# Giving every room a length that is a multiple of 128 bytes, and a planner's durations taken from the trace

## The chip, the cores and the metric

The kernel runs on one core of one Trainium2 chip. The metric is the device time of one execution in microseconds (us); lower is better. An execution is one launch that computes the whole reference.

## The reference

Two macaron layers over x, 256 tokens by 1024 features, all in float32. Each layer is a SwiGLU feed-forward, a mixer, and a second feed-forward, each closed by a LayerNorm. The mixer is a bidirectional mLSTM in layer 0 and a windowed attention in layer 1.

```python
def swiglu(x, w_in, w_out):            # w_in 1024 x 5632, w_out 2816 x 1024
    gu = x @ w_in
    g, u = gu[..., :D_FF], gu[..., D_FF:]
    return (jax.nn.silu(g) * u) @ w_out

for l in range(2):
    x = layer_norm(ALPHA * x + 0.5 * swiglu(x, ffn_w_in[l, 0], ffn_w_out[l, 0]), ...)
    y = mlstm_mixer(x, ...) if l == 0 else window_attention(x, ...)
    x = layer_norm(ALPHA * x + y, ...)
    x = layer_norm(ALPHA * x + 0.5 * swiglu(x, ffn_w_in[l, 1], ffn_w_out[l, 1]), ...)
```

Nearly all of the work is in four feed-forwards of 256 tokens with 17.3 million weights each.

## The kernel before, in words

**Products.** Each float32 matrix is split in two parts that TensorE takes as float32r: `hi`, the value rounded by a cast on ScalarE (ACT), and `lo`, the rest, by a subtraction on VectorE (DVE). A product is three matmuls (`mm3`): hi·hi, hi·lo, lo·hi. In nearly all of them the weights are the moving operand, 128 x 512 (`w_hi`, `w_lo`), and the activations are the stationary one, 128 x 128: `xT_hi`/`xT_lo` (the transposed x), `h_hi`/`h_lo` and `hc` (the gated activations, called h), `q` (the attention's output) or `S` (sums of blocks of x). The text calls a matmul with 512 moving columns a long product. There are 3447 of them among TensorE's 4459 matmuls.

**Feed-forward.** Columns of `w_in` are taken in blocks. A first block is computed plainly from `xT`; then four calls of `seven`, in which seven block products stand for eight (a Strassen-like scheme: sums of weight blocks are made by DVE and by DMAs that add, issued by GpSimd, POOL). A call of `seven` has 84 long products, 36 of them with `xT` and 48 with `S`, and up to 48 of the down projection (`py<-w,h`), 132 together in the first three of the four calls, 108 in the last, and 8 transposes. Then `tail` does the last of the down projection, the residual and the LayerNorm (`Norm`): half of token tile 1 is computed while tile 0 is normalized, and tile 1 is normalized while the next stage starts.

**Order.** No engine's order is written by hand. `Book` records every step. TensorE keeps the recorded order. For the other queues (ACT, DVE, POOL, and SP, which issues the loads) `sequence` simulates the program: each step has a duration (`takes`) and a time until its result is seen (`later`), both set in `cost`; a step gets a due time from TensorE's order, and the most urgent one that can start is taken.

**Rooms.** SBUF is cut into rooms of the kinds in `HOMES`: (bytes per partition, number of rooms). A step that opens a room waits for a free one of its kind. `hi` and `lo` hold the split weights, 10 each; `big` holds raw weights as loaded, h, S and v; `small` holds statistics. Each room becomes one tile, allocated when it is first used, so that a room's address is the sum of all the lengths before it. The constants `xT_hi` and `xT_lo` stand at bytes 24704 and 32896 of a partition, multiples of 128. Behind them stand the small constants (`mhalf`, `gcol`, `gw`, `gbias`, `sink`, `neg_sink`), 736 bytes in all, and among the rooms small ones of 32 to 96 bytes. Rooms that hold `v` (128 x 4 x 258, 4128 bytes) are not a multiple of 128 long either.

In the built program this is where the operands of the 3447 long products begin, as the remainder of the byte modulo 128:

| moving, stationary | before | after |
|---|---|---|
| 96 and 0 | 1408 | |
| 96 and 96 | 1135 | |
| 96 and 32 | 273 | |
| 32 and 96 | 214 | |
| 32 and 0 | 192 | |
| 96 and 64 | 160 | |
| 32 and 32 | 41 | |
| 32 and 64 | 24 | |
| 0 and 0 | | 3447 |

Before, the two remainders are equal in 1176 long products and differ in 2271; all 1536 long products with `xT` are among the latter.

The program's own scheduling function is the place of the durations that change:

Of the kernel before, what the change touches and what calls it, by code (L numbers as in the profile page):

```python
# [10 lines left out]
F32 = mybir.dt.float32  # L11
# [7 lines left out]
S = 256  # L19
# [6 lines left out]
A = slice(None)  # L26
# [2 lines left out]
HOMES = {  # L29
    "hi": (4096, 10),  # L30
    "lo": (4096, 10),
    "big": (4128, 20),
    "wide": (4352, 2),
    "temp": (2048, 6),
    "small": (80, 20),
# [73 lines left out]
class View:  # L109
# [27 lines left out]
    def real(self):  # L137
        r = self.room.real
        for name, args, kw in self.ops:
            r = getattr(r, name)(*args, **kw)  # L140
        return r
# [23 lines left out]
class Book:  # L165
# [76 lines left out]
    def cost(self, s):  # L242

        size = lambda v: int(np.prod(v.shape[1:]))
        n = max([size(v) for v in s.outs + s.ins], default=0)
        if s.engine == "PE":
            n = size(s.outs[0])
            s.takes, s.later = (109.0 if s.name == "transpose" else n / 2.4 + 13.3), 200.0
            if s.name == "matmul" and s.args[1].shape[0] == 64:
                s.takes = 111.0  # L250
        elif s.name == "dma_start":
            s.takes = {"SP": ISSUE, "ACT": 480.0, "POOL": 1250.0}[s.engine]
            s.later = 0.0
        elif s.engine == "DVE":
            s.takes, s.later = (n + 71) / 0.96, 120.0
            if s.name == "tensor_tensor_scan":
                s.takes = 700.0
            if s.name == "tensor_tensor_reduce":
                s.takes += 60.0
        elif s.engine == "ACT":  # L260
            s.takes, s.later = n * 0.912 + 25.0, 125.0
            if s.name.startswith("preload"):
                s.takes = 1290.0
            if s.name == "activation" and s.args[2] is not AF.Copy:
                s.takes += 30.0
            if "accum_out" in s.kw:
                s.takes += 100.0
        else:
            s.later = 150.0
            s.takes = {"tensor_tensor": 1500.0, "tensor_add": 1000.0, "partition_broadcast": 1100.0, "iota": 600.0,  # L270
                       "affine_select": 1000.0}.get(s.name, n * 0.93 + 60.0)
            if s.name == "tensor_add" and n >= 512:
                s.takes = 2150.0

    def seen(self, s):
        return s.end + s.later
# [148 lines left out]
    def emit(self):  # L425
        nc = self.nc
        engines = {"PE": nc.tensor, "DVE": nc.vector, "ACT": nc.scalar, "POOL": nc.gpsimd, "SP": nc.sync}
        real = lambda x: x.real() if isinstance(x, View) else x
        for s in self.order():
            for r in s.rooms:  # L430
                if r.real is None:
                    pool = self.pools[r.kind == "bank"]
                    r.real = pool.tile(list(r.shape), r.dtype, name=r.name, tag=f"{r.kind}{r.slot}", bufs=1)
            getattr(engines[s.engine], s.name)(*[real(x) for x in s.args], **{k: real(x) for k, x in s.kw.items()})  # L434

# [2 lines left out]
def trunk_kernel(ctx: ExitStack, tc: tile.TileContext, x, ffn_w_in, ffn_w_out, ln_g, ln_b, ml_w_in, ml_gate_b,  # L438
                 ml_norm_g, ml_w_out, at_w_in, at_sink, at_w_out, out):
    consts = ctx.enter_context(tc.tile_pool(name="consts", bufs=1))  # L440
    rooms = ctx.enter_context(tc.tile_pool(name="rooms", bufs=1))
    banks = ctx.enter_context(tc.tile_pool(name="banks", bufs=1, space=bass.MemoryType.PSUM))
    ctx.enter_context(tc.manual_schedule())
    nc = Book(tc.nc, (rooms, banks))

    stages = [("ffn", 0, 0, 0), ("mlstm", 0, 0, 1), ("ffn", 0, 1, 2),
              ("ffn", 1, 0, 0), ("attn", 1, 0, 1), ("ffn", 1, 1, 2)][:STAGES]
# [1 line left out]
    def const(name, shape, dtype=F32):  # L449
        t = consts.tile(list(shape), dtype, name=name)  # L450
        v = nc.tile(name, shape, "const", dtype)
        v.room.real = t
        v.room.slot = 0
        return v
# [4 lines left out]
    def pair(p, *idx):  # L459
        return p[0][idx], p[1][idx]  # L460

    def bank(shape=(128, 512), name="pw"):
        return nc.tile(name, shape, "bank")
# [4 lines left out]
    def small(name, shape):  # L468
        return nc.tile(name, shape, "small")

    def both(name, shape, kind="big"):
        return tuple(nc.tile(name + e, shape, kind, FR) for e in ("_hi", "_lo"))
# [50 lines left out]
    def mm3(o, l, r, start, stop, onto=False):  # L523
        nc.tensor.matmul(o, l[0], r[0], start=start, stop=False, skip_group_check=onto)
        nc.tensor.matmul(o, l[0], r[1], start=False, stop=False, skip_group_check=onto)
        nc.tensor.matmul(o, l[1], r[0], start=False, stop=stop, skip_group_check=onto)
# [11 lines left out]
    xt = [const(f"x{t}", [128, D]) for t in range(2)]  # L538
    xT = tuple(const("xT" + e, [128, 8, S], FR) for e in ("_hi", "_lo"))
    ident = const("ident", [128, 128])  # L540
    mhalf = const("mhalf", [128, 2])
    gcol = const("gcol", [128, 8])
    gw = const("gw", [128, 8, 16])
    gbias = const("gbias", [128, 1])
    sink = const("sink", [128, 16])
    neg_sink = const("neg_sink", [128, 16])

    for t, h in ((0, 0), (1, 0), (0, 1), (1, 1)):
        s_ = slice(h * 512, h * 512 + 512)
# [120 lines left out]
    def ffn(l, i, n, pending, last):  # L670
        wi, wo = ffn_w_in[l, i], ffn_w_out[l, i]
        hT, y = {}, []
        start = pending is None

        def h_room(width):
            if width == 4:
                return both("h", (128, 4, S))
            v = nc.tile("hc", (128, 2, 2, S), "big", FR)
            return v[:, 0], v[:, 1]

# [81 lines left out]
        def x_four():  # L762
            x_sum("S4", turned[0, 1], OP.add, f1["S2"])

        hB = h_room(4)
        chunks(hB, 4)
        hB0 = hB
# [59 lines left out]
        def seven(g, before):  # L827
# [7 lines left out]
            of = lambda k0, t: (lambda k: pair(xT, A, k0 + k, tok(t)))  # L835
            sum_ = lambda name: (lambda k: pair(xs[name], A, k))
            hB = h_room(4)
            chunks(hB, 4)
            qa, qc = bank(), bank()
# [61 lines left out]
        for t in range(2):  # L901
            sg = temp("sg")[:, 0:256]
            nc.scalar.activation(sg, ps[t][:, 0:256], AF.Silu)
            hh.append(temp("hh")[:, 0:256])
            nc.vector.tensor_mul(hh[t], sg, ps[t][:, 256:512])
        hp = h_room(2)
        chunks(hp, 2)
        down(1)
# [17 lines left out]
        return tail(y, lambda c, t: pair(hT[c], A, tok(t)), (todo, todo), False, norm, last, 4, turn)  # L926

    def mlstm(l, n, pending, last):
        va = [both(f"v{t}", (128, 4, 258)) for t in range(2)]
        gwi = both("gw", (128, 8, 128))  # L930
        for p in gwi:
            nc.gpsimd.memset(p.bitcast(F32), 0.0)
# [44 lines left out]
        for d in range(2):  # L977
            q = slice(32 * d, 32 * d + 32)
# [4 lines left out]
        for d in range(2):  # L983
            q = slice(32 * d, 32 * d + 32)
# [39 lines left out]
        for m in range(2):  # L1024
            for g in range(2):
                pieces = [narrow(ml_w_in[0], a * 512, 512 * m + 256 * g) for a in range(2)]
                p = bank((128, 2, S))
# [10 lines left out]
        am = {}  # L1038
# [17 lines left out]
        def mix(h):  # L1056
            den = small("den", (128, 2, 2))
            ys = []
            for t in range(2):
                for d in range(2):  # L1060
                    y = bank(name="py")
                    terms = [(t, t)] if t == d else [(t, t), (2, 1 - t)]
                    for n_, (blk, sb) in enumerate(terms):
                        mm3(y[:, 0:258], pair(am[h], A, d, blk), pair(va[sb], A, h), n_ == 0, n_ == len(terms) - 1)
                    nc.scalar.activation(den[:, t, d:d + 1], y[:, 256:257], AF.Abs)
                    ys.append(y)
            part[h] = den, ys
# [42 lines left out]
        for h in range(4):  # L1110
            wide_mm(po[h // 2], 0, wg, h // 2, range(4 * (h % 2), 4 * (h % 2) + 4))
            scores(h)
            if h:
                mix(h - 1)
                divide(h - 1)
                settle(h - 1)
        po1 = [bank(), bank()]
        sigm(0, 0, po[0])
        wide_mm(po1[0], 1, wg, 0, range(4))
        mix(3)  # L1120
        sigm(0, 1, po[1])
        wide_mm(po1[0], 1, wg, 0, range(4, 8))
# [12 lines left out]
        y = [[bank(name="py") for _ in range(2)] for _ in range(2)]  # L1135
# [10 lines left out]
    def attn(l, n, pending, last):  # L1146
# [18 lines left out]
        va = [nc.tile(f"v{t}", (128, 17, 64), "wide", FR) for t in range(2)]  # L1165
        for t in range(2):
            nc.gpsimd.memset(va[t][:, 0:17:2].bitcast(F32), 0.0)
        kT = both("kT", (128, 4, S))
        qh = [both(f"q{h}", (128, 4, S)) for h in range(2)]
        qT = lambda j, *idx: pair(qh[j // 4], idx[0] if idx else A, j % 4, *idx[1:])  # L1170
        kd, qd = [], []
        wkq = later([lambda c0=c0, a=a: wide(at_w_in[0], a * 256, c0) for c0 in (1024, 0) for a in range(4)])
# [99 lines left out]
        y = []  # L1272
# [53 lines left out]
    for j, (kind, l, i, n) in enumerate(stages):  # L1326
        last = j == len(stages) - 1
        bound[0] = j
        if kind == "ffn":
            pending = ffn(l, i, n, pending, last)  # L1330
        elif kind == "mlstm":
            pending = mlstm(l, n, pending, last)
        else:
            pending = attn(l, n, pending, last)
# [30 lines left out]
```

## Time and profile before

| | |
|---|---|
| median of 3 runs | 941.18 us (941.17 to 941.67) |
| profiled execution | 941.73 us, its span 940.0 us |
| granted TensorE clock | 0.998 |
| TensorE (PE) busy | 919.6 us, 98% |
| VectorE (DVE) busy | 809.6 us, 86% |
| ScalarE (ACT) busy | 584.0 us, 62% |
| GpSimd (POOL) busy | 155.6 us, 17% |
| moved by DMA | 208.54 MB, mean 222 GB/s |

The profile's page gives the busy time of the engines; PEld is the weight load of TensorE (the stationary operand), which overlaps its matmuls (PE). A matmul's record ends about 0.39 us after its start, though the next one starts 0.23 us after it: matmuls overlap in the array. So the cost of a matmul is read from start to start, or from the chain of work, whose pieces are laid end to end. Line numbers in the profile are nearly all L434, the line of `emit` that issues every step; names tell the steps apart.

### The profile page before, as it was taken

What the parts mean: (1) busy time and instruction counts of PE and PEld (TensorE: products, weight loads), DVE (VectorE), ACT (ScalarE), POOL (GpSimd) and SP (SyncE); (2) the same over time, 40 slices, a digit from 0 to 9 for tenths busy, and PEclk for the clock granted to TensorE, in tenths of its full rate; (3) what the DMA queues carried; (4) which work ended last, traced back from release to release, by engine and by line L of the source; (5) the groups of instructions that cost most, each with busy time, mean ns of one, the idle gap of its engine ahead of it and who ended that gap; (6) DMA issues with size and microseconds to landing.
All of it is one profiled execution on the core that took longest, in us unless ns stands there. A gap on an engine that the chain in (4) does not pass through costs nothing.

```text
span 940.0 us, 12633 instructions
## 1 busy us (share of the span) xinstructions
PE 919.6 (98%) x4459; PEld 756.4 (80%) x4459; DVE 809.6 (86%) x969; ACT 584.0 (62%) x793; POOL 155.6 (17%) x194
## 2 busy tenths in 40 slices
PE   8999999999999999999999999999989999999997
PEld 6888888789978888888878888887878878888885
DVE  6979999887788979999789799988776688899975
ACT  6676767548454666676446676675467555776660
POOL 6112111015011012111011112110045302111100
PEclk9999999999999999999999999999999999999999
DMA  9998999854296488988975889988522457989821
GB/s 315 334 258 197 286 283 274 289 183 143 104 369 221 132 211 217 305 275 220 335 246 135 240 215 272 303 264 286 172 74 79 157 202 158 281 241 236 270 46 45
DMA packets 100704, 208.54 MB, mean 222 GB/s; under 512 B 6904, under 2 KB 21264, under 8 KB 100640
## 3 DMA queue, kind: packets, MB, share of 16 engines
q1 hardware_dynamic: 82368, 173.04, 53.2%
q0 software_dynamic: 17696, 33.65, 21.0%
q10 hardware_dynamic: 576, 1.05, 0.3%
q8 instruction: 35, 0.57, 0.3%
q14 instruction: 29, 0.24, 0.1%
HBM read 206.65 MB, written 1.05 MB: 221 GB/s over the span
## 4 chain that ended last, share of the span: by engine, by line
PE 84%; DVE 8%; DMA 3%; issue 2%; ACT 2%; POOL 1%; DVEq 0%; SPq 0%; ACTq 0%; POOLq 0%
PE pw L434 56%; PE py L434 27%; DVE w_lo L434 4%; DMA raw<-in_ffn_w_in_dram 1%; DMA raw<-in_ml_w_in_dram 1%; DVE x L434 1%; ACT w_hi L434 1%; ACT sc L434 1%; DMA raw<-in_ffn_w_out_dram 0%; POOL rs L434 0%; DVE stats L434 0%; DVE b L434 0%; DVE xT_lo L434 0%; DVE sc L434 0%; DVE e L434 0%
## 5 line engine op out<-in xcount | busy, mean ns | idle before, releaser
L434 ACT CAST w_hi<-b 128x1024 fp32r<-128x1024 f32 x224 | 234.1, 1053 | 93.5 <-PE py L434 53.4
L434 DVE TENSOR_TENSOR w_lo<-b,w_hi 128x1024 fp32r<-128x1024 f32 x224 | 267.5, 1219 | 25.4 <-ACT w_hi L434 25.2
L434 ACT CAST w_hi<-raw 128x1024 fp32r<-128x1024 f32 (+1 forms) x181 | 186.8, 1046 | 101.5 <-PE py L434 65.9
L434 DVE TENSOR_TENSOR w_lo<-raw,w_hi 128x1024 fp32r<-128x1024 f32 (+1 forms) x181 | 216.8, 1214 | 33.8 <-ACT w_hi L434 33.3
L434 PE MATMUL pw<-w_hi,xT_hi 128*128 128x512 f32 x480 | 192.1, 401 | 0.1
L434 PE MATMUL pw<-w_hi,xT_lo 128*128 128x512 f32 x480 | 189.4, 396 | 2.8 <-DVE xT_lo L434 2.8
L434 PE MATMUL pw<-w_lo,xT_hi 128*128 128x512 f32 x480 | 189.0, 395 | 1.3 <-DVE w_lo L434 1.3
L434 PE MATMUL pw<-w_hi,S 128*128 128x512 f32 x512 | 164.6, 392 | 0.0
L434 POOL DMA_DIRECT2D b<-in_ffn_w_in_dram x64 | 77.3, 1210 | 465.9 <-DVE b L434 161.4
L434 PE MATMUL py<-w_hi,h_hi 128*128 128x512 f32 x317 | 126.2, 398 | 0.0
L434 PE MATMUL py<-w_hi,h_lo 128*128 128x512 f32 x317 | 124.8, 394 | 0.4 <-DVE h_lo L434 0.4
L434 PE MATMUL py<-w_lo,h_hi 128*128 128x512 f32 x317 | 124.5, 393 | 0.0
L434 PEld LDWEIGHTS pw<-w_hi,S 128*128 128x128 f32 x512 | 96.1, 188 | 21.7
L434 PEld LDWEIGHTS pw<-w_hi,xT_lo 128*128 128x128 f32 x480 | 90.1, 188 | 25.9 <-DVE xT_lo L434 4.5
L434 PEld LDWEIGHTS pw<-w_lo,xT_hi 128*128 128x128 f32 x480 | 90.2, 188 | 21.6 <-DVE w_lo L434 1.7
L434 PEld LDWEIGHTS pw<-w_hi,xT_hi 128*128 128x128 f32 x480 | 90.1, 188 | 20.2 <-ACT w_hi L434 0.6
L434 PE MATMUL pw<-w_lo,S 128*128 128x512 f32 x256 | 100.4, 392 | 0.0
L434 DVE TENSOR_TENSOR b<-b,b 128x1024 f32<-128x1024 f32 x64 | 78.0, 1221 | 1.2
L434 PEld LDWEIGHTS py<-w_hi,h_lo 128*128 128x128 f32 x317 | 59.5, 188 | 14.9 <-DVE h_lo L434 1.1
L434 PEld LDWEIGHTS py<-w_lo,h_hi 128*128 128x128 f32 x317 | 59.6, 188 | 13.0
L434 PEld LDWEIGHTS py<-w_hi,h_hi 128*128 128x128 f32 x317 | 59.6, 188 | 12.6
L434 PEld LDWEIGHTS pw<-w_lo,S 128*128 128x128 f32 x256 | 48.1, 188 | 10.9
(198 smaller groups left out, 1083.1 us busy)
## 6 DMA issues: line engine op xcount, KB each, us to landing
b<-in_ffn_w_in_dram SPq DMA_DIRECT2D x128, 512.0 KB, 6.4
raw<-in_ffn_w_out_dram SPq DMA_DIRECT2D x88, 512.0 KB, 6.8
b<-in_ffn_w_in_dram POOLq DMA_DIRECT2D x64, 512.0 KB, 8.1
raw<-in_ffn_w_in_dram SPq DMA_DIRECT2D x32, 512.0 KB, 7.6
raw<-in_ml_w_in_dram SPq DMA_DIRECT2D x24, 512.0 KB, 6.1
raw<-in_ffn_w_in_dram SPq DMA_DIRECT2D x32, 256.0 KB, 7.3
raw<-in_at_w_in_dram SPq DMA_DIRECT2D x12, 512.0 KB, 8.8
raw<-in_ml_w_out_dram SPq DMA_DIRECT2D x8, 512.0 KB, 4.1
```

The costliest lines, as they stand in the source:

```text
L434: getattr(engines[s.engine], s.name)(*[real(x) for x in s.args], **{k: real(x) for k, x in s.kw.items()})
```

## The change

It has three parts.

1. Rooms. Kinds of length 4128 go: `big` has 16 rooms of 4096 bytes, and a new kind `tall` has 4 of 4224 (33 x 128). `tall` holds h of width 4, v of the mLSTM (now 264 columns a head, of which 258 are read) and q of the attention. The six small constants become parts of one tile `few` of 768 bytes. Small rooms get a pool of their own (`smalls`), allocated behind all the others.
2. Durations in `cost` for DVE, ACT and POOL, which set the order of their queues. None of an instruction's own shape, type or work changes.
3. What follows: the order of DVE, ACT and POOL, and which room a step gets.

TensorE's order and the order of the loads on SP are as before.

```diff
 HOMES = {
     "hi": (4096, 10),
     "lo": (4096, 10),
-    "big": (4128, 20),
+    "big": (4096, 16),
+    "tall": (4224, 4),
     "wide": (4352, 2),
...
         elif s.engine == "DVE":
+            psum = any(v.room.kind == "bank" for v in s.ins)
             s.takes, s.later = (n + 71) / 0.96, 120.0
+            if s.name == "scalar_tensor_tensor":
+                s.takes += 55.0
+            if psum and s.outs[0].dtype is F32:
+                s.takes += 60.0
             if s.name == "tensor_tensor_scan":
-                s.takes = 700.0
+                s.takes = 710.0
             if s.name == "tensor_tensor_reduce":
-                s.takes += 60.0
+                s.takes = 490.0
+            if s.name == "bn_stats":
+                s.takes = 728.0 if n == 512 else 335.0
...
         elif s.engine == "ACT":
-            s.takes, s.later = n * 0.912 + 25.0, 125.0
+            s.takes, s.later = n * 0.912 + 17.0, 125.0
...
-                    pool = self.pools[r.kind == "bank"]
+                    pool = self.pools[{"bank": 1, "small": 2}.get(r.kind, 0)]
...
-    mhalf = const("mhalf", [128, 2])
-    gcol = const("gcol", [128, 8])
-    gw = const("gw", [128, 8, 16])
...
+    few = const("few", [128, 192])
+    gw = few[:, 0:128].rearrange("p (k g) -> p k g", k=8)
+    gcol, sink, neg_sink = few[:, 128:136], few[:, 136:152], few[:, 152:168]
+    mhalf, gbias = few[:, 168:170], few[:, 170:171]
...
-                return both("h", (128, 4, S))
+                return both("h", (128, 4, S), "tall")
...
-        va = [both(f"v{t}", (128, 4, 258)) for t in range(2)]
+        va = [both(f"v{t}", (128, 4, 264), "tall") for t in range(2)]
...
-        qh = [both(f"q{h}", (128, 4, S)) for h in range(2)]
+        qh = [both(f"q{h}", (128, 4, S), "tall") for h in range(2)]
```

The order moves little. Two places are shown. The first is DVE's queue where the third feed-forward follows the second (the same happens behind the first feed-forward and where the attention follows the third feed-forward). `x_66` and `x_67` (after: `x_69`, `x_70`) are token tiles 0 and 1; `xT_lo` is the lo part of the transposed tile 0, which TensorE needs for the first products of the next stage. Before:

```order
L434 SCALAR_TENSOR_TENSOR x_66<-x_66,rs,ln_b 128x1024
L434 TENSOR_TENSOR w_lo<-raw,w_hi 128x1024 x2
L434 SCALAR_TENSOR_TENSOR x_67<-x_67,py 128x512
L434 BN_STATS stats<-x_67 128x6
L434 TENSOR_TENSOR w_lo<-raw,w_hi 128x1024
L434 TENSOR_TENSOR xT_lo<-py,xT_hi 128x4x128 x2
L434 SCALAR_TENSOR_TENSOR x_67<-x_67,py 128x512
```

And after:

```order
L448 SCALAR_TENSOR_TENSOR x_69<-x_69,rs,ln_b 128x1024
L448 TENSOR_TENSOR w_lo<-raw,w_hi 128x1024 x2
L448 SCALAR_TENSOR_TENSOR x_70<-x_70,py 128x512
L448 BN_STATS stats<-x_70 128x6
L448 TENSOR_TENSOR xT_lo<-py,xT_hi 128x4x128 x2
L448 SCALAR_TENSOR_TENSOR x_70<-x_70,py 128x512
```

One subtraction of a weight, `w_lo`, no longer stands directly ahead of `xT_lo`; it comes later in the queue. Behind the attention one of the two `w_lo` ahead of tile 1's residual moves up, and the one ahead of `xT_lo` stays.

The second place is POOL's queue in the first feed-forward. Here the two elements at the end of each row of v are set (`v_hi`, `v_lo`), which opens v's rooms. Before, at the start of the program:

```order
L434 DMA gbias<-in_ml_gate_b_dram 4x1 x4
L434 MEMSET ones 64x1
L434 MEMSET v_hi 128x4x2
L434 MEMSET v_lo 128x4x2
L434 MEMSET v_hi 128x4x2
L434 MEMSET v_lo 128x4x2
L434 DMA gcol<-in_ml_norm_g_dram 128x8x1
```

After, at the end of the first feed-forward, between the two powers of its LayerNorm (`rs`, tile 0 and tile 1):

```order
L448 TENSOR_TENSOR rs<-rs,few 128x1
L448 MEMSET v_hi 128x4x2
L448 MEMSET v_lo 128x4x2
L448 MEMSET v_hi 128x4x2
L448 MEMSET v_lo 128x4x2
L448 TENSOR_TENSOR rs<-rs,few 128x1
L448 DMA most<-scan 4x256 x2
```

v's four rooms are no longer held through the first feed-forward; they are opened when h's last rooms come free.

More of the change, by code (lines that the diff above doesn't have):

```diff
@@ L254, in cost @@
         elif s.engine == "DVE":
+            psum = any(v.room.kind == "bank" for v in s.ins)
             s.takes, s.later = (n + 71) / 0.96, 120.0
+            if s.name == "scalar_tensor_tensor":
+                s.takes += 55.0
+            if psum and s.outs[0].dtype is F32:
+                s.takes += 60.0
             if s.name == "tensor_tensor_scan":
-                s.takes = 700.0
+                s.takes = 710.0
             if s.name == "tensor_tensor_reduce":
-                s.takes += 60.0
+                s.takes = 490.0
+            if s.name == "bn_stats":
+                s.takes = 728.0 if n == 512 else 335.0
+            if s.name == "bn_aggr":
+                s.takes = 244.0 if n > 6 else 115.0
         elif s.engine == "ACT":
-            s.takes, s.later = n * 0.912 + 25.0, 125.0
+            s.takes, s.later = n * 0.912 + 17.0, 125.0
             if s.name.startswith("preload"):
@@ L264, in cost @@
             if s.name == "activation" and s.args[2] is not AF.Copy:
-                s.takes += 30.0
+                s.takes += 48.0
+            if any(isinstance(s.kw.get(k), View) for k in ("bias", "scale")):
+                s.takes += 110.0
             if "accum_out" in s.kw:
-                s.takes += 100.0
+                s.takes += 93.0
         else:
             s.later = 150.0
[L270 to L273, printed above, removed]
+            s.takes = {"tensor_tensor": 1500.0, "partition_broadcast": 1100.0, "iota": 600.0,
+                       "affine_select": 1000.0}.get(s.name, n * 0.93 + 100.0)
+            if s.name == "tensor_add":
+                s.takes = 2150.0 if n >= 512 else 1000.0
+            if s.name == "tensor_scalar":
+                s.takes = 460.0
     def seen(self, s):
@@ L441, in trunk_kernel @@
     rooms = ctx.enter_context(tc.tile_pool(name="rooms", bufs=1))
+    smalls = ctx.enter_context(tc.tile_pool(name="smalls", bufs=1))
     banks = ctx.enter_context(tc.tile_pool(name="banks", bufs=1, space=bass.MemoryType.PSUM))
     ctx.enter_context(tc.manual_schedule())
-    nc = Book(tc.nc, (rooms, banks))
+    nc = Book(tc.nc, (rooms, banks, smalls))
     stages = [("ffn", 0, 0, 0), ("mlstm", 0, 0, 1), ("ffn", 0, 1, 2),
@@ L540, in trunk_kernel @@
     ident = const("ident", [128, 128])
-    mhalf = const("mhalf", [128, 2])
-    gcol = const("gcol", [128, 8])
-    gw = const("gw", [128, 8, 16])
-    gbias = const("gbias", [128, 1])
-    sink = const("sink", [128, 16])
-    neg_sink = const("neg_sink", [128, 16])
+    few = const("few", [128, 192])
+    gw = few[:, 0:128].rearrange("p (k g) -> p k g", k=8)
+    gcol, sink, neg_sink = few[:, 128:136], few[:, 136:152], few[:, 152:168]
+    mhalf, gbias = few[:, 168:170], few[:, 170:171]
     for t, h in ((0, 0), (1, 0), (0, 1), (1, 1)):
@@ L1063, in mix @@
                     for n_, (blk, sb) in enumerate(terms):
-                        mm3(y[:, 0:258], pair(am[h], A, d, blk), pair(va[sb], A, h), n_ == 0, n_ == len(terms) - 1)
+                        mm3(y[:, 0:258], pair(am[h], A, d, blk), pair(va[sb], A, h, slice(0, 258)), n_ == 0, n_ == len(terms) - 1)
                     nc.scalar.activation(den[:, t, d:d + 1], y[:, 256:257], AF.Abs)
```

## The prediction

> **What bounds the kernel now.** I read the page first, then the chain of work in order of time, then who waited for whom.
>
> ```profile
> span 940.0 us, 12633 instructions
> PE 919.6 (98%) x4459; PEld 756.4 (80%) x4459; DVE 809.6 (86%) x969; ACT 584.0 (62%) x793; POOL 155.6 (17%) x194
> PE 84%; DVE 8%; DMA 3%; issue 2%; ACT 2%; POOL 1%; DVEq 0%; SPq 0%; ACTq 0%; POOLq 0%
> ```
>
> TensorE is busy for 98% of the span and is 84% of the chain that ended last. So the time is the sum of the steps from one matmul's start to the next one's, plus a few waits. The profiled execution took 941.73 us, 1.73 outside its span; the median of the runs is 941.18, 0.55 below it.
>
> The chain's pieces show what a step costs (start, length, what, number of matmuls):
>
> ```profile
> 75.26 3.23 PE pw L434 x16
> ...
> 106.56 3.24 PE pw L434 x16
> ...
> 118.56 2.72 PE py L434 x12
> ...
> 344.97 2.80 PE py L434 x12
> ...
> 364.50 3.24 PE pw L434 x16
> ...
> 427.50 3.24 PE pw L434 x16
> ...
> 488.89 24.65 PE pw L434 x110
> ...
> 544.41 3.24 PE pw L434 x16
> 547.65 2.76 PE py L434 x12
> ...
> 607.10 3.23 PE pw L434 x16
> ...
> 813.01 5.44 PE pw L434 x24
> ...
> 821.23 3.23 PE pw L434 x16
> ...
> 883.98 3.23 PE pw L434 x16
> ```
>
> Set beside the bytes at which the built program's operands begin, these tell the change's whole matter. At 813.01 all 24 long products have both operands at 96 modulo 128: 5.44 / 24 = 226.7 ns a step. At 118.56 all but one of twelve do: 2.72 / 12 = 226.7. At 344.97 the same instructions, py<-w,h, take 2.80 / 12 = 233.3; there h_hi begins at 64 and w_lo at 32, so that 7 of the 12 differ. At 488.89 stand 102 long products with xT, moving at 96 or 32 and stationary at 0, all different, and 8 transposes at 0.109: (24.65 - 0.87) / 102 = 233.1 ns. At 547.65 all twelve are equal again, but they come right behind transposes: 2.76. There the steps take some 230 ns at first and settle at 227 after about six. So a step costs 226.7 ns where the bytes are equal and have been for a while, and 233 where they differ.
>
> **The change part by part: the step.** After the change all 3447 long products have both operands at 0. The page has the number of those with xT; they are 480 x 3, and 32 x 3 more stand in the mLSTM's output projection.
>
> ```profile
> L434 PE MATMUL pw<-w_hi,xT_hi 128*128 128x512 f32 x480 | 192.1, 401 | 0.1
> L434 PE MATMUL pw<-w_hi,xT_lo 128*128 128x512 f32 x480 | 189.4, 396 | 2.8 <-DVE xT_lo L434 2.8
> L434 PE MATMUL pw<-w_lo,xT_hi 128*128 128x512 f32 x480 | 189.0, 395 | 1.3 <-DVE w_lo L434 1.3
> L434 PE MATMUL py<-w_hi,xT_hi 128*128 128x512 f32 x32 | 12.8, 401 | 0.0
> ```
>
> 1536 x (233.1 - 226.7) = 9.8 us. For the other 1911, with S, h, hc or q, I take one call of `seven`. The pieces x16 come once a call: 75.26 to 106.56, 364.50 to 427.50 (two), 544.41 to 607.10 (two), 821.23 to 883.98 (two) are 219.74 us for seven calls, 31.39 each. Less 8 transposes (0.87) and 36 products with xT (8.39), 22.13 us stay for 96 products, 230.5 ns each. 1911 x (230.5 - 226.7) = 7.3 us. Together 17.1 us. The settling stays: by PE's order the long products come in about 75 runs, broken by transposes, short products or a wait, and 547.65 against 118.56 prices a break at 0.04 us: 3.0 us. This leaves **14.1 us**.
>
> What the trace does not show is a long product with both operands at 0. Its nearest rows are those with both at 96, 226.7, and with stationary at 0 and moving at 96, 233.1. If equality is what counts, it is the first; if the place of the stationary operand alone did it, it would be the second, and the gain 0, or, all products slowing to 233.1, a loss of 1911 x 2.6 = 5.0 us. Against the second stand the steps in runs of at least eight long products with one pair throughout, counted from PE's rows: moving 96 with stationary 32 (37 steps) or 64 (23) takes 232 to 233, as 0 does (503 steps, 233.3), and 96 with 96 takes 227.2 (347 steps). Three places of the stationary operand are slow and the one that equals the moving operand's is fast. I take 226.7.
>
> The other products gain nothing that I can see: 256 columns take about 117 ns with equal and with different bytes, transposes 109. I cost them at nothing.
>
> **Who must keep up.** A faster TensorE uses up weights faster. The waits say who pushes:
>
> ```profile
> ACT w_hi L434 <- PE py L434: 119.2, 73, 5.6
> DVE w_lo L434 <- ACT w_hi L434: 58.8, 96, 4.5
> PE pw L434 <- DVE w_lo L434: 1.3, 1, 1.3
> SPq L434 <- DVE w_lo L434: 446.1, 218, 15.7
> 545.00:576.00 31.00, 31.00 (x140) 25.30 (x139) 29.68 (x30) 21.75 (x26) 4.81 (x4) 1.00 0.93 257
> ```
>
> TensorE waited for a w_lo once, at the start. ACT waits for TensorE to free `hi` rooms, SP for DVE to free `big` rooms: the supply is held back, not late. In a stretch as long as a call (last row: PE, PEld, DVE, ACT, POOL, clock, DMA share, GB/s) DVE is busy 29.68 of 31 us. A call needs 29.68 x 31.39 / 31 = 30.1 us of DVE; TensorE will need about 31.39 - 132 x (231.2 - 226.7) / 1000 + settling, some 30.9. DVE stays below it, by 0.8 us a call instead of 1.3; DMA's share goes from 0.93 to 0.95. Cost nothing, by that cover.
>
> **Rooms.** Before, 20 `big` rooms held h and, through the whole first feed-forward, v; after, h and v use 4 `tall` ones and 16 are left. In the first feed-forward this frees rooms for loads; later it takes away the rooms that h left idle, up to two pairs. SP's queue waits for rooms 446 us in all, so loads are issued later there; they stay ahead as long as ACT keeps waiting for TensorE and not for a load. I cost it at nothing; a bound is given with the rival.
>
> **Order at the stage boundaries.** Behind the first feed-forward, the second, the third and the attention, TensorE waits for xT_lo. At the second of these, and at the last (755.25), the rows read:
>
> ```profile
> 476.16 1.07 ACT L434 CAST xT_hi<-py 128x512 fp32r<-128x512 f32 x2
> 476.58 1.21 DVE L434 TENSOR_TENSOR w_lo<-raw,w_hi 128x1024 fp32r<-128x1024 f32 x1
> 477.70 1.28 DVE L434 TENSOR_TENSOR xT_lo<-py,xT_hi 128x512 fp32r<-128x512 f32 x2
> 478.44 0.50 PE L434 MATMUL pw<-w_hi,xT_lo 128*128 128x512 f32 x1 [0.54 <-DVE xT_lo L434]
> 755.25 0.50 PE L434 MATMUL pw<-w_hi,xT_lo 128*128 128x512 f32 x1 [1.13 <-DVE xT_lo L434]
> PE pw L434 <- DVE xT_lo L434: 2.8, 4, 1.1
> ```
>
> xT_hi's first half is there at about 476.7, so xT_lo could start 0.9 us earlier if w_lo did not stand ahead of it. The new order puts w_lo behind it at three boundaries, and behind the attention leaves one w_lo of two on the way. The four waits are 2.8 us; I take **2.2** off (between 0 and 2.8). The w_lo that moves back is late by 1.2 us and has `lo` rooms of lead before TensorE uses it.
>
> **POOL.** The four memsets of v, now between the two powers of the first LayerNorm, must wait for TensorE's last use of h. The second power needs DVE's residual, statistics and sum behind that same use, over 1.5 us of work; four memsets take less. Nothing, or 0.3 us at worst. `few` lies on no path: all its loads are issued at the start as before.
>
> **What is given back.** Where something other than TensorE ends last, its gain is lost. In the attention TensorE is idle for 7.7 us of 88:
>
> ```profile
> 668.00:756.00 88.00, 80.32 (x536) 68.28 (x534) 62.43 (x131) 59.05 (x139) 29.46 (x49) 1.00 0.39 121
> ```
>
> Of its 144 long products' 0.8 us I count all as lost, and 0.5 us for the products that cover the LayerNorms: **1.3 us**. The new order of DVE and ACT within the attention can go either way; of 7.7 us idle I would not believe more than 3 in either direction, and take 0.
>
> Sum: 14.1 + 2.2 - 1.3 = 15.0 us. 941.73 - 15.0 = 926.7 for a profiled execution, 926.2 for the median: **926**.
>
> **A rule against it.** The rows at 813.01 and 488.89 differ by 6.4 ns a step. The Trainium skill, in "TensorE: Matmul & The Clock Gate", section "Part 2: What happens when you issue a matmul", says that TensorE reads the moving operand and the weights through two independent ports, and that loading the next weights takes no bandwidth from the running matmul. By this rule the bytes of the one could not matter to the other, and the 14.1 us would be 0. The trace doesn't agree: the same instruction on the same shapes takes 226.7 or 233 with nothing else in PE's queue changed.
>
> **The rivals.** First, the step does not change: something that only went along with the bytes makes it, such as which rooms h and S stand in. Then only the order counts: 941.2 - 2.2 and up to 3 of the attention either way, 936 to 942, about 939. For it: no pair at 0 has been seen. Against it: steps change within a run of equal instructions as the room changes. The two ports of which the Trainium skill speaks, above, would give this result.
>
> Second, the step shortens but the supply doesn't follow: DVE, 30.1 us a call by the row at 545, gets less done in the new order, and eats 0.3 to 0.6 us in each of 16 calls. 926 + 5 to 10: 931 to 936. Against it: ACT's 119 us of waiting for rooms.
>
> Third, slower: too few `big` rooms. If loads come so late that ACT waits for them and the ten split pairs run out, TensorE stops. It decides at about 0.94 us of stop in each of the 16 calls (15.0 / 16); at 1.2 us the time is 926 + 19 = 945. For it: 16 rooms for 20 and a DMA share of 0.93. Against it: v's and h's rooms come out of the 20 as well, so a feed-forward loses at most the pairs that h left free.
>
> **How the numbers follow.** The forecast, 920 to 931, has 0.71: it takes in 0 to 2.8 at the boundaries, 3 either way in the attention, and 12.5 to 17.1 for the step. The supply rival has 0.14, no change of the step 0.09, slower 0.06. The range of 8 in 10 runs from 920 to 934; it takes in the forecast and most of the second. A measurement of this kernel can tell about 0.2%, 1.9 us, from no change. Faster by more than that: 0.71, 0.14 and 0.04 of the first rival, 0.89. Within: 0.04 of it. Slower: 0.07.
>
> **What would show it.** In the chain after: py x12 pieces of 2.72 to 2.76 everywhere, pw x24 of 5.44 to 5.47, and the piece of 102 products with xT near 24.0 instead of 24.65. Calls 30.8 to 30.9 us apart. PE's wait for xT_lo below 1 us in all. ACT still waiting for TensorE, not for loads. The prediction is wrong if pieces of 2.80 stay (first rival), if PE waits for w_lo appear in the feed-forwards (second), or ACT's waits for DMA grow (third).

## The result, and the profile after

The kernel after takes 926.88 us (median of 4 runs, 926.79 to 926.94), the kernel before, beside it, 941.42 (4 runs, 941.17 to 941.67). The ratio is 0.9845, with a 95% interval of 0.9828 to 0.9863: 1.5% faster. The forecast was 926, with a range of 920 to 934. The sum came out, but two of its terms did not: the steps gave half of what was forecast, and the order gave what they lacked.

The page after, in the lines that were shown of before (span, busy time of each engine, shares of the chain):

```profile
span 925.2 us, 12627 instructions
PE 910.2 (98%) x4459; PEld 758.0 (82%) x4459; DVE 809.8 (88%) x969; ACT 584.5 (63%) x793; POOL 155.2 (17%) x194
PE 93%; DVE 3%; ACT 2%; issue 1%; DMA 1%; DVEq 0%; SPq 0%; ACTq 0%
```

TensorE is still the bound. Its busy time fell by 9.4 us of the 14.8 by which the span fell; the other 5.4 were time without a matmul. The chain in order of time (start, length, what, number of matmuls):

```profile
482.44 24.14 PE pw L448 x110
...
798.88 5.44 PE pw L448 x24
804.32 2.72 PE py L448 x12
807.04 3.16 PE pw L448 x16
...
818.90 2.81 PE py L448 x12
...
838.21 3.16 PE pw L448 x16
```

The piece of 102 products with xT went from 24.65 to 24.14 us, not quite to the 24.0 foreseen. The x24 pieces, products with S, are at 5.44 or 5.45. But the down projection `py<-w,h` did not get faster: 2.81 us for 12 products, as slow as the slowest of before, although h and w now begin at the same byte modulo 128. The py piece at 804.32, at 2.72, is the one with `hc` of that call. So a call of `seven` took 31.17 us (807.04 to 838.21), where 30.8 to 30.9 was foreseen and 31.39 measured before.

TensorE's waits, a wait that shows the supply, and the two stretches that were shown of before (a call, and the attention; columns PE, PEld, DVE, ACT, POOL, clock, DMA share, GB/s):

```profile
PE pw L448 <- DVE nm L448: 3.0, 4, 0.9
PE py L448 <- DVE xT_lo L448: 0.4, 1, 0.4
ACT w_hi L448 <- PE py L448: 117.4, 71, 5.5
535.00:566.00 31.00, 31.00 (x141) 25.50 (x140) 29.86 (x30) 22.18 (x26) 4.81 (x4) 1.00 0.94 274
658.00:744.00 86.00, 81.85 (x550) 70.58 (x549) 63.27 (x133) 58.63 (x139) 28.19 (x49) 1.00 0.40 129
```

The row `PE pw <- DVE xT_lo` (2.8 us in four waits) is gone; the 0.4 that stays is in the tail of the mLSTM. ACT still waits 117 us for TensorE to free rooms: the supply follows, in DVE's 29.86 of 31 us too. In the attention TensorE is idle 4.15 us where it was 7.7; the prediction had taken 0 for the order there.

For a sum, PE's matmuls were joined with the bytes at which the built program puts their operands, and the steps from one start to the next averaged by stationary operand (steps under 300 ns, from 25 us on, in ns):

```
                    xT     S, hc   h, q   256 columns, w
(count)            1536     864    1047    288
before             232.9   230.4   231.0   119.6
after              228.0   226.9   233.0   122.0
```

Times the counts: xT -7.4 us, S and hc -3.0, h and q +2.1, the short products +0.7; together **-7.6 us**. What single steps took beyond the usual one of their number of columns (those over 80 ns more) fell from 22.9 to 15.5 us, **-7.4**: the attention -3.5, the four boundaries -3.7, the mLSTM's tail +0.4, the rest -0.6. The two make 15.0, and the span fell by 14.8.

### The profile page after: what moved, and what is told of

Same layout as the page of the kernel before. It is cut to its first block, busy times and chain, and to the rows that moved or that the text cites. A ratio compares the mean times of both kernels' runs of the same rounds, so it can differ in the third digit from the quotient of the medians.

```text
span 925.2 us, 12627 instructions
## 1 busy us (share of the span) xinstructions
PE 910.2 (98%) x4459; PEld 758.0 (82%) x4459; DVE 809.8 (88%) x969; ACT 584.5 (63%) x793; POOL 155.2 (17%) x194
## 4 chain that ended last, share of the span: by engine, by line
PE 93%; DVE 3%; ACT 2%; issue 1%; DMA 1%; DVEq 0%; SPq 0%; ACTq 0%
PE pw L448 59%; PE py L448 33%; DVE w_lo L448 1%; DMA raw<-in_ffn_w_in_dram 1%; ACT w_hi L448 1%; ACT sc L448 1%; DVE x L448 0%; DVE h L448 0%; DVE stats L448 0%; DVE q_lo L448 0%; DVE xT_lo L448 0%; DVE sc L448 0%; DVE hst L448 0%; ACT q_hi L448 0%; DVE S L448 0%
## 5 line engine op out<-in xcount | busy, mean ns | idle before, releaser
L448 ACT CAST w_hi<-raw 128x1024 fp32r<-128x1024 f32 (+1 forms) x181 | 187.0, 1047 | 99.6 <-PE py L448 69.0
L448 PE MATMUL pw<-w_hi,xT_hi 128*128 128x512 f32 x480 | 189.4, 396 | 0.0
L448 PE MATMUL pw<-w_lo,xT_hi 128*128 128x512 f32 x480 | 186.6, 390 | 1.2 <-DVE w_lo L448 1.2
L448 PE MATMUL pw<-w_hi,xT_lo 128*128 128x512 f32 x480 | 187.0, 391 | 0.0
```

## The experiments

Two theories of the slow h products stood against each other. In the kernel after, all rooms of `hi`, `lo` and `big` and both parts of xT begin at 128 modulo 256. The tall rooms are 33 x 128 bytes long, so every second of them begins at 0 modulo 256, and of each pair h_hi, h_lo one part does. *Modulo 256*: the bytes must be equal modulo 256. *Modulo 128*: they are as they should be, and h is slow for another reason, its bank or its place at the end of memory. For the order there were two more: *A*, rooms and durations act each by itself; *B*, the number of rooms of each kind makes the order too.

### The bytes: tall4352, small12, few896, sweep, few736

**tall4352** makes the tall rooms 17 x 256 bytes long, and takes 12 small rooms to have the place:

```diff
-    "tall": (4224, 4),
+    "tall": (4352, 4),
...
-    "small": (80, 20),
+    "small": (80, 12),
...
-        va = [both(f"v{t}", (128, 4, 264), "tall") for t in range(2)]
+        va = [both(f"v{t}", (128, 4, 272), "tall") for t in range(2)]
```

> The four tall rooms are 4352 bytes long (17 x 256) instead of 4224 (33 x 128), and 12 small rooms make place for them; every engine's order is that of the kernel after. All 3447 long products now begin with both operands at the same byte modulo 256; before this edit 943 (all of h and q but a few) did not, though all were equal modulo 128. Theory 'modulo 256' (a long product takes 226.9 ns a step only if both operands begin at the same byte modulo 256, otherwise 233.3): the 1047 products with h or q fall from a mean of 233.2 to 226.9, so -5.8 to -6.6 us: 920.6 us (919.8 to 921.6); pieces py x12 at 2.72 to 2.75 us (now 2.77 to 2.81). Theory 'modulo 128' (my prediction's; the slow h products have another cause, their bank or their place at the end of SBUF): 926.9 us, py x12 as now.

**small12** has the second of these three edits alone.

> The kernel after with 12 small rooms instead of 20, nothing else; the order is the same on every engine. A control for the run with tall rooms of 4352 bytes. Both theories: 926.9 us within 0.7, py x12 at 2.77 to 2.81.

Measured: tall4352 921.39 us (5 runs, 921.2 to 924.07; to before 0.9778, interval 0.9758 to 0.9797), small12 926.89 (4 runs, 926.81 to 926.95; 0.9826, interval 0.981 to 0.9843). The difference is 5.5 us, with every engine's order the same. The page and the chain of tall4352:

```profile
span 919.7 us, 12634 instructions
...
802.59 3.16 PE pw L448 x16
...
814.43 2.72 PE py L448 x12
...
833.47 3.16 PE pw L448 x16
```

The py pieces with h are at 2.72 to 2.77, and a call takes 30.88 us, within the 30.8 to 30.9 that the prediction gave for equal bytes. The 1047 steps with h and q fell from 233.0 to 227.7 ns: 5.6 us. In the kernel after, 618 of these 1047 products are themselves unequal modulo 256; the 943 of the expectation are about those that are unequal or stand right before one that is (942). *Modulo 128* is out.

**few896** and **few736** change the length of the one tile that lies between xT and the rooms, and so move all rooms against xT and nothing else:

```diff
-    few = const("few", [128, 192])
+    few = const("few", [128, 224])     # few896: w against xT at 128 modulo 256
+    few = const("few", [128, 184])     # few736: at 224 modulo 256, 96 modulo 128
```

> The constants tile few is 896 bytes long instead of 768, so that all rooms lie 128 bytes further on while xT stays: w and xT are still equal modulo 128 and now differ by 128 modulo 256, in all 1536 long products with xT; w against h, q, S and hc is as it was, and so is the order. Theory 'modulo 256': 1536 x (233.3 - 226.9) = +9.8 us: 936.7 (935 to 938), pw x24 from 5.44 to 5.58-5.62. Theory 'modulo 128': 926.9, pw x24 5.44.

> The constants tile few is 736 bytes long instead of 768, so that all rooms lie 32 bytes nearer and xT stays: w and xT differ by 224 modulo 256 (96 modulo 128), as before the change; all else and the order as after. Of the 1536 long products with xT only. Theory 'modulo 256': as with few896, 933.6 us, but the products with 256 columns and w go back from 122 to 119.6 ns (-0.7): 932.9 (932 to 934.5). Theory 'modulo 128 has a part of its own': slower than few896 by 2 us or more.

Measured: few896 933.58 us (4 runs, 932.79 to 934.35; 0.9897, interval 0.988 to 0.9915), few736 933.07 (4 runs, 933.04 to 934.55; 0.9902, interval 0.9887 to 0.9917). Of the chain of few896, the piece that was 24.14 after, then an x24 and a py piece:

```profile
485.80 24.64 PE pw L448 x110
...
828.79 5.45 PE pw L448 x24
834.23 2.81 PE py L448 x12
```

Equal modulo 128 and different modulo 256 is as slow as different in both: 24.64 is what before had (24.65). Of few896's expectation two details were missed. The loss is 6.7 us and not 9.8, because a step with xT went from 228.0 to 232.6 on average, not from 226.9 to 233.3: xT's products stand in short runs, and the steps behind a break are slow with equal bytes too. I had expected the x24 pieces to slow; they are products with S, which lies in the rooms beside w and moved with it.

few736 was to bring the short products back to 119.6 ns. Their average was 124.5, and 124.4 in few896, but this is not the bytes: in both profiled executions TensorE's granted clock is halved for 3.4 us in the attention, and 17 and 13 short products in a row take some 213 ns there. In few896, before and during the stretch:

```profile
678.90:682.30 3.40, 1.81 (x15) 1.13 (x14) 3.38 (x6) 1.11 (x3) 0.00 (x0) 1.00 1.03 363
682.30:685.70 3.40, 3.36 (x15) 3.14 (x16) 1.30 (x6) 2.56 (x10) 0.11 (x1) 0.50 0.69 236
```

Outside it they average 119.2 ns in few736 and 120.6 in few896, beside 122.0 after and 119.6 before: few736's expectation came true. The two executions of few896 with a mean clock of 0.996 took 934.30 and 934.35 us, the two at 0.998 and 0.999 932.86 and 932.79, so the stretch costs some 1.5 us where it comes.

**sweep** measures the rule by itself: runs of 36 products in a row at chosen distances.

```
for name, pattern, cols in RUNS:          # ("d128s", [(0, 128)], 512), ...
    for g in range(3):
        ...
        for k in range(12):
            a, b = pattern[k % len(pattern)]         # bytes of the moving, of the stationary operand
            a = a // 4 + 1024 * (k // 3 % 2) + 512 * (k % 2)
            b = b // 4 + 8192 + 1024 * (k // 3 % 4) + 256 * (k % 2)
            nc.tensor.matmul(y[:, 0:cols], w[:, b:b + 128], w[:, a:a + cols], start=k == 0, stop=k == 11)
```

> No trunk: runs of 36 long products (float32r, 128x128 stationary, 128x512 moving) with nothing to wait for, one run for each distance in bytes between the two operands (d0 to d2048), for both moved together, for one or two of every three products at distance 128, and three runs of 256 columns. The output is not the reference's. Theory 'modulo 256': 36 x 226.9 = 8.17 us for d0, d256, d512, d768, d1024, d2048 and for both moved together; 36 x 233.3 = 8.40 for all other distances, d128, d384 and d640 among them; one of three unequal: two slow steps of three, 8.32. Theory 'modulo 128': d128, d384, d640 and the mixed runs at 8.17 too. Of 256 columns: 120 ns a step if equal, 117 if not.

Its chain, each piece 36 products (the number in a name is the stationary operand's distance in bytes; `mv128s`: the moving one's):

```profile
20.85 8.17 PE d0s L45 x36
29.02 8.39 PE d32s L45 x36
...
54.23 8.37 PE d128s L45 x36
...
71.00 8.24 PE d192s L45 x36
...
87.63 8.17 PE d256s L45 x36
95.80 8.37 PE d384s L45 x36
...
153.34 8.37 PE dfour L45 x36
...
186.49 8.21 PE bothb128s L45 x36
194.70 8.37 PE mv128s L45 x36
203.07 8.24 PE mv64s L45 x36
211.32 8.32 PE one_of_three L45 x36
...
236.41 8.24 PE one_of_six L45 x36
244.66 4.31 PE shortsame L45 x36
248.97 4.27 PE shortby128s L45 x36
253.24 4.22 PE shortby96s L45 x36
```

Multiples of 256 take 226.9 ns a step, 128 and 384 take 232.5, and 4 bytes already cost as much. Moving both operands together costs nothing in the end (the last 24 of `bothb128s` take 226.9 each). Only 192 bytes, at 228.9, lie between, which neither theory has; the moving operand 64 bytes on (`mv64s`, the same distance modulo 256) takes as long. Where one product of three is at 128, its steps repeat as 232, 234, 227; where one of six is, as 226, 227, 227, 226, 233, 234. So an unequal product slows its own step and the one before it. The py products after follow this. Where h_hi is the unequal part (237 of 317 times), two products of three are unequal and all three steps are slow, 233 to 234 ns; where h_lo is (80 times), its step and the one before take 234 and 232, and the third 228. At 256 columns equality costs a little instead: 119.7 ns equal, 118.6 at 128, 117.2 at 96.

### Rooms or durations: rooms_only, durations_only, tall_old_durations

**rooms_only** is the kernel after with the planner's durations of before (all lines of the change that set `s.takes` undone). **durations_only** is the kernel before with those lines alone. **tall_old_durations** is tall4352 with the durations of before.

> The rooms of the kernel after (big 16, four tall rooms, few, small rooms in a pool of their own) with the durations of the kernel before, so that DVE stands almost as before (905 of 969 instructions in the same place by name). What the two traces hold of steps: products with xT -5.8 us, with S and hc -3.0, with h and q +2.5, 256 columns with w +0.8, in sum -5.5. Theory A (the rooms bring the steps, the durations bring the order, each by itself): 941.4 - 5.5 = 935.9 us (934.5 to 937.5), and the excess over the usual step, mostly at the stage boundaries, stays near 16 us. Theory B (the rooms' counts set the order as well): below 932, with waits near 9 us.

> The rooms of the kernel before with the durations of the kernel after, nothing else; DVE stands almost as after (913 of 969 by name). Theory A: the order's part, 7.5 us, and some 1 to 2 us because 285 more long products happen to be equal modulo 256: 941.4 - 9 = 932.4 us (930.5 to 935); PE waits 2.8 us less for xT_lo at the four boundaries. Theory B: 938 to 941.

> The kernel with tall rooms of 4352 bytes, all 3447 long products equal modulo 256, with the durations of the kernel before: beside tall4352 (921.4 us) it shows what the order alone is worth where no step can differ. Theory A: +7.5 us: 928.9 (927 to 931). Theory B: +1 to +3.

Measured: rooms_only 933.95 us (4 runs; 0.9911, interval 0.9893 to 0.9929), durations_only 935.49 (4 runs; 0.9921, interval 0.9906 to 0.9937), tall_old_durations 929.19 (4 runs; 0.9871, interval 0.9841 to 0.9901). The kernel before took 942.8 us beside these, 0.15% more than beside after, so I compare profiled spans: 940.0 before, 932.4 with the rooms alone (-7.6), 933.6 with the durations alone (-6.4), 925.2 with both (-14.8). Where no step can differ, the order is worth 929.19 - 921.39 = 7.8 us. That is theory A: each part brings its own, and 0.8 of 14.8 is left over (less than what a stretch of halved clock, told next, cost the profiled execution of durations_only). My expectation for rooms_only was 2 us too high, since I had summed the steps without their counts; the means times counts above give the 7.6. For durations_only it was 3 us too low. Its profiled execution, too, has a granted clock of 0.50 for 3.4 us, from 683.7 on in the attention; three of its executions, with a mean clock of 0.996, took 935.30 to 935.78 us, and the one at 0.998 took 934.07, within the range. That stretch also raised the average of the short products to 124.7 ns (119.5 outside it). And the pairs that became equal by chance gave less than the 1 to 2 us expected: the steps with S went from 230.4 to 229.6 ns, 0.7 us, and xT stayed at 232.8.

### Which part of the order: reduce_only, stt_only, dve_only

All three start from tall_old_durations, where all long products are equal, so that a change in time is one of waits.

```diff
             if s.name == "tensor_tensor_reduce":
-                s.takes += 60.0
+                s.takes = 490.0                              # reduce_only
...
+            if s.name == "scalar_tensor_tensor":             # stt_only
+                s.takes += 55.0
```

dve_only has all of the change's lines for DVE and none for ACT and POOL.

> Beside tall_old_durations (929.2 us, tall rooms of 4352 bytes, the durations of before): only the duration of DVE's tensor_tensor_reduce is that of after, 490 ns. In DVE's order this moves nothing but the attention's stretch (places 701 to 749 of 969: the sums sc and nm come earlier, w_lo and q_lo later); the four boundaries stay with w_lo ahead of xT_lo. Between the two kernels with tall rooms of 4352 bytes the steps of PE over their usual time shrink by some 3.2 us in the attention and 4.6 at the boundaries, and the tail of the mLSTM is 0.1 worse. Theory 'the attention's gain is this one order': 929.2 - 3.2 = 926.0 us (925.3 to 927). Theory 'it came from the boundaries, or from ACT's order': 929.2 (within 0.7).

> Beside tall_old_durations (929.2 us): only the 55 ns more on DVE's scalar_tensor_tensor. In DVE's order this moves w_lo behind xT_lo at the last boundary alone (near 744 us), where PE's step over its usual time is 1.49 + 0.11 us in that kernel and 0.11 in the one with the durations of after; two w_lo change places near 190 us, and two turns at the end. Theory 'a w_lo ahead of xT_lo costs what PE's step shows there': 929.2 - 1.5 = 927.7 us (927.2 to 928.3). Theory 'only the wait shown for xT_lo counts' (1.3 us, less the 0.2 that I took off in each): 928.1. If the time comes back later: 929.2.

> Beside tall_old_durations (929.2 us): all of DVE's durations are those of after, ACT's and POOL's those of before. All four boundaries and the attention's stretch move; 905 of 969 DVE instructions stand where they stand with all durations of after. Theory 'DVE's durations are the whole order's gain': 921.4 us (920.8 to 922.5). Theory 'ACT's bring a part of it': 923 to 925.

Measured: reduce_only 926.78 us (4 runs, 926.64 to 926.97; 0.9832, interval 0.9817 to 0.9846), stt_only 928.87 (4 runs, 928.11 to 929.84; 0.9857, interval 0.9841 to 0.9874), dve_only 925.37 (4 runs, 924.81 to 926.84; 0.9819, interval 0.9804 to 0.9834). TensorE's waits in tall_old_durations, then in reduce_only:

```profile
PE pw L435 <- DVE nm L435: 4.7, 7, 0.9
PE pw L435 <- DVE xT_lo L435: 3.4, 4, 1.3
```

```profile
PE pw L435 <- DVE nm L435: 3.9, 5, 1.0
PE pw L435 <- DVE xT_lo L435: 3.3, 4, 1.3
```

One number in the planner, which moves DVE's instructions, and with them ACT's, within the attention alone, is worth 2.4 us; two of seven waits for nm, the scores' maxima, are gone, and the boundaries are as they were. It isn't the 3.2 that I had counted from steps: dve_only, below, has no more of it, so the rest needs ACT's or POOL's durations.

At the last boundary DVE does this in tall_old_durations, and then in stt_only (start, length, what; in brackets TensorE's wait):

```profile
740.06 2.36 DVE L435 TENSOR_TENSOR w_lo<-raw,w_hi 128x1024 fp32r<-128x1024 f32 x2
...
743.66 1.21 DVE L435 TENSOR_TENSOR w_lo<-raw,w_hi 128x1024 fp32r<-128x1024 f32 x1
744.78 1.28 DVE L435 TENSOR_TENSOR xT_lo<-py,xT_hi 128x512 fp32r<-128x512 f32 x2
745.52 0.50 PE L435 MATMUL pw<-w_hi,xT_lo 128*128 128x512 f32 x1 [1.33 <-DVE xT_lo L435]
```

```profile
740.27 1.22 DVE L437 TENSOR_TENSOR w_lo<-raw,w_hi 128x1024 fp32r<-128x1024 f32 x1
...
742.73 1.21 DVE L437 TENSOR_TENSOR w_lo<-raw,w_hi 128x1024 fp32r<-128x1024 f32 x1
743.85 1.28 DVE L437 TENSOR_TENSOR xT_lo<-py,xT_hi 128x512 fp32r<-128x512 f32 x2
...
744.59 0.50 PE L437 MATMUL pw<-w_hi,xT_lo 128*128 128x512 f32 x1 [0.18 <-DVE xT_lo L437]
```

Three w_lo stood between x and xT_lo, and one has left; my expectation had it going behind xT_lo, but the one directly ahead stays. The wait fell by 1.15 us, PE's steps there from 1.60 beyond the usual to 0.45, and the span from 927.3 to 926.4. The medians (929.19 and 928.87, each with runs over a range as wide as the difference) can't show it; the profile does.

dve_only removes all four boundary waits (TensorE's list has no xT_lo at all) and has the attention of reduce_only, and yet it is 4.0 us above tall4352. The wait that took their place stands in the tail of the mLSTM:

```profile
PE py L444 <- DVE h L444: 2.1, 1, 2.1
```

Its chain there:

```profile
265.18 1.16 ACT w_hi L444
266.34 1.28 DVE w_lo L444
267.62 0.34 DVE h L444
```

DVE's `w_lo` stands ahead of the h on which TensorE waits, and itself waits for ACT's `w_hi`. PE's steps beyond the usual are 3.9 us there, in tall4352 1.5: some 1.6 us more for the wait, and 0.9 for a halved clock behind it (last section). The durations for ACT and POOL, undone here, are worth these 2.4 us and some 1.2 in the attention. The first theory, that DVE's are the whole gain, fell.

## Why the prediction was right and wrong

- **Step, 14.1 us forecast, 7.6 measured.** The mechanism was right, its modulus wrong: "where the bytes are equal" was read modulo 128, and it is modulo 256. h and q, in tall rooms of 33 x 128 bytes, went up by 2.1 us instead of down by some 4. tall4352 shows the rest by its 5.5 us, and then the calls are 30.88 us apart. By the prediction's own sign (pieces of 2.80 that stay) the forecast of the step failed for h. The trace of before could have told: nearly all its pairs that are equal modulo 128 are equal modulo 256 too, 1153 of 1176, so my rows at 813.01 and 118.56 couldn't tell the two apart; but seven steps with moving and stationary equal and the next weights 128 bytes off took 233.9 ns, and I had not grouped by more than 128.
- **Settling, 3.0 us taken off.** Even in tall4352 xT's steps are at 228.0 and h's at 227.7 ns, against 226.7 settled: 1536 x 1.3 + 1047 x 1.0 = 3.0 us. That term was right.
- **Short products at nothing.** They cost 0.7 us: their steps went from 119.6 to 122.0 ns on average, and sweep has 119.7 with equal bytes against 117.2 at 96. The trace of before has no product of w and xT in which the bytes are equal.
- **Boundaries, 2.2 forecast (at most 2.8), 3.7 measured.** The waits of 2.8 us went away in full, the last one too, since one of the w_lo ahead left. And the steps at a wait take more than the wait: 1.60 us beyond the usual where 1.33 was waited in tall_old_durations. I had taken something off where I should have added.
- **Attention, order at 0, and 1.3 us given back.** It gained 3.5, 2.4 of it by the duration of one instruction (reduce_only), and of what the steps gained nothing was seen to be lost: tall4352 got its 5.5 us of 5.6. I had not followed the order of DVE within the attention at all, and had put 3 us either way for it, which was 0.5 too narrow; only the range of the sum held.
- **POOL, rooms, `few`, supply, at nothing.** The runs agree: small12 is within 0.01 us, rooms_only gains what its steps say with 16 `big` rooms, ACT waits for TensorE as before.
- **Rivals.** "The step does not change" fell: the steps with xT and S did, and sweep shows it without any rooms. The rule of two ports that the Trainium skill gives ("TensorE: Matmul & The Clock Gate", "Part 2: What happens when you issue a matmul") has no place for a difference by the bytes, and sweep shows one of 5.6 ns in 227: the same products take 8.17 us at distance 256 and 8.37 at 128. Whether the ports are the cause was not shown. "The supply doesn't follow" and "too few rooms" did not come.

So 926 was met by luck, since two misses cancelled: 6.5 us too much for the steps, and 6.5 too little for the order (7.4 for 0.9, boundaries less what was given back). tall4352, the change with its rooms made multiples of 256, is what the prediction of the step described, and is the fastest kernel measured here: 921.39 us.

## What to carry to other kernels

Before an alignment rule is taken from a trace, group the steps by twice and four times the modulus too, and look for the few pairs that differ in the last of them; where none exist, say which modulus the trace can't tell apart. Before an average of steps is put down to the bytes, read the granted clock of the stretches in it: here 13 products in one of 3.4 us moved the average of 288. A sum can be right with two wrong terms: give each term a row that would show it, as the py pieces did here. Where one shared tile lies between two groups of operands, its length is a free experiment on their distance, with the order untouched.

## What the runs showed of the hardware

A float32r product of 512 columns takes 226.9 ns a step when moving and stationary operand begin at the same byte modulo 256, and 232 to 234 at the other distances measured (228.9 at 192); the slow step is that of the unequal product and of the one before it. Why was not shown.

A wait can cost more than its length, since TensorE's granted clock can be halved behind it. In dve_only, behind the 2.12 us in which TensorE waited for h, the clock is 0.50 for 3.4 us, and the products begin 0.43 us apart for six steps and more, and 0.23 from 272.48 on:

```profile
269.10:272.50 3.40, 3.40 (x12) 2.72 (x10) 2.88 (x5) 0.79 (x2) 0.00 (x0) 0.50 0.92 244
```

```profile
268.82 0.88 PE L444 MATMUL py<-ident,h 128*128 128x128 f32 x4 [2.12 <-DVE h L444]
...
269.92 0.63 PE L444 MATMUL pw<-w_lo,xT_hi 128*128 128x512 f32 x1
270.35 0.63 PE L444 MATMUL pw<-w_hi,xT_lo 128*128 128x512 f32 x1
...
272.48 0.39 PE L444 MATMUL py<-w_lo,xT_hi 128*128 128x512 f32 x1
```

A stretch of the same length came behind waits of 0.95 to 1.01 us in the profiled executions of few896, few736 and durations_only; tall_old_durations waited 1.33 us at its last boundary and kept a clock of 1.00. What decides was not shown.

The Trainium skill, in "TensorE: Matmul & The Clock Gate", "Part 1: The HAM clock gate (the "warmup" mystery)", gives 426.7 ns a step at 512 columns for a cold array, which these 427 ns match, and about 3.4 us of idling until it gets cold. Here less was enough: in few896 TensorE was busy for 1.81 of the 3.4 us before its clock was halved. The section's 215.7 ns for a warm array isn't seen in any run here: the fastest settled steps of these float32r products are 226.7.
